# A hybrid decoder layer: part of the 128x128 transposes turned in 32x32 blocks by VectorE and moved by SBUF transfers

## The chip, the cores and the metric

The kernel runs on one core of a Trainium2 chip. Times are device microseconds (us) of one execution. Engines: PE is TensorE, PEld its weight loads, DVE is VectorE, ACT is ScalarE, POOL is GpSimd, SP is SyncE, whose queue issues nearly all transfers of this kernel. L12 is line 12 of the profiled kernel.

## The reference

One layer over 2048 positions of width 1024. Two head groups run side by side on the same projections: four HGRN2 heads (a gated linear recurrence in chunks) and eight attention heads in a sliding window of 128 with a sink logit. Their outputs are concatenated and projected, and a gated MLP with a causal convolution and a last RMSNorm follow. What the change touches:

```python
f = lb + (1.0 - lb) * sigmoid(hf);  log_f = log(f);  k_hg = 1.0 - f
o_hg = hgrn2_chunkwise(q_hg, k_hg, v_hg, log_f)        # per head, 128 keys, 128 values
o_hg = rmsnorm(o_hg, hg_norm_w) * silu(hg)
# attention: block n of 128 queries reads key blocks n-1 and n
dist = qi + ATT_BLOCK - kj;  band = (dist >= 0) & (dist < WINDOW)
p = exp(scores - m);  denom = sum(p) + exp(sink - m)
out = einsum('bnhgqk,bnkhd->bnqhgd', p / denom, vb)
mix = concatenate([o_hg, o_att]);  h = h + mix @ w_out
```

Since the window equals the block, a query sees of its own block the keys up to its own position, and of the previous block exactly the keys after that position: the two masks are complements.

## The kernel before

The 2048 positions go in two halves of 1024. In each, a mix stage (heads, attention) is followed by the output projection, gate and up, and down. Activations lie with features on the 128 partitions and time along the row. Every large product is made of three TensorE matmuls, from a rounded high part and a low part of both factors; a unit of 48 matmuls of 512 columns (8 slices of the width x 3 x two blocks of 512) makes one 128-wide projection for the half. Weights come through three `raw` buffers; ScalarE rounds them to `whi`, VectorE makes the rest `wlo`, two buffers each.

**Attention.** Heads go in four pairs j (one of each key head kv), each pair in two groups g of 512 queries. Stage `qa` projects the queries; `sc` makes the scores `psc`, puts both key blocks into one tile `sc` of 128 keys per query (previous block copied by ScalarE, L405 and L407, own block laid over it by VectorE under the mask `own`, L408), takes the maximum (L411), Exp with sums (L421) and scales (L426). Stages `pv` and `pw` are the value products of group 0 and 1: eight TensorE transposes `ppt` (L435, four for each kv) bring keys onto the partitions, VectorE writes them twice, under the masks `ownT` and `prevT` (L438), and `poT` (L446) sums V of the own block times the one and V of the previous block times the other.

**Heads.** For head h, stage `f` projects and takes Tanh, `q` projects the queries and makes f (VectorE, L472), `l` makes K = 1 - f (VectorE, L475) and works through seven levels of blocks of 1, 2, .. 64 positions (`pdiag`, `plev`), `s` makes the states, `p` the output `po`: ScalarE squares it out of PSUM (L604), VectorE scales it (L612), TensorE transposes it (`pot`, L617, eight for each head), and stage `g` multiplies the gate. Stages `m` split the finished rows into the operands of the output projection.

**Order.** The string `ORDER` gives the sequence in which the stages are traced. A scheduler then places every instruction on its engine by its own estimates and sets the semaphores; each engine, and SyncE's queue, runs its list in order. Tiles of one tag share a number of buffers, and an instruction waits until its buffer is free. A transfer also waits for the eighth transfer before it, whose semaphore it takes.

Of the kernel before, what the change touches and what calls it, by code (L numbers as in the profile page):

```python
# [39 lines left out]
ORDER = ("f0 q0 l0 qa0 v0 s0 p0 sc0 f1 q1 l1 pv0 pw0 qa1 s1 p1 sc1 f2 q2 l2 pv1 pw1 qa2 v1 s2 p2 sc2 f3 q3 l3 "  # L40
         "pv2 pw2 qa3 sc3 s3 p3 g0 pv3 pw3 g1 m4 m5 m6 g2 m0 m1 g3 m7 m2 m3").split()
# [4 lines left out]
VB = 2  # L46


@with_exitstack
def hymba_layer(ctx: ExitStack, tc: tile.TileContext, a: dict, out: bass.AP, rows_out: bass.AP):  # L50
# [29 lines left out]
    ones = cp.tile([P, P], F32, name="ones")  # L80
    nc.vector.memset(ones, 1.0)
# [3 lines left out]
    nc.scalar.activation(warm, ones[:, 0:1], AF.Tanh)  # L85
# [5 lines left out]
    kc = cp.tile([P, 2, P], F32R, name="kcarry")  # L91
    vc = cp.tile([P, P], F32, name="vcarry")
# [6 lines left out]
    def constants():  # L99
# [3 lines left out]
        C.prevT = cp.tile([P, P], F32, name="prevT")  # L103
        for t, op, sgn in ((C.own, ALU.is_ge, 1), (C.ownT, ALU.is_ge, -1), (C.prevT, ALU.is_gt, 1)):
# [229 lines left out]

    def rows(kv):
        return slice(kv * HD, (kv + 1) * HD)

    def att_keys(hf, kv, invb, p):

        KS = p.tile([P, 2, P + HALF], F32R, name="KS")
        V = p.tile([P, 1 + TT, P], F32, name="V")
        if hf:
            nc.vector.tensor_copy(KS[:, :, 0:P], kc)
            nc.vector.tensor_copy(V[:, 0], vc)
        kT, vT = [p.tile([P, HALF], F32, tag="f", name=n, bufs=2) for n in ("kT", "vT")]
        for jj, dst in ((ATT_J, kT), (ATT_J + 1, vT)):
            o = kv[jj - ATT_J]  # L350
            for b, bs in halves():
                nc.vector.tensor_tensor(blocks(dst[:, bs], b), blocks(o[b]), blocks(invb[:, bs]), op=ALU.mult)
                nc.scalar.activation(dst[:, bs], dst[:, bs], AF.Identity, bias=C.battn[:, jj:jj + 1])
        for kv in range(2):
            r, other = rows(kv), rows(1 - kv)
            nc.scalar.copy(KS[r, kv, P:], kT[r])
            nc.vector.tensor_tensor(KS[other, kv, P:], kT[r], KS[r, kv, P:].bitcast(F32), op=ALU.subtract)
        for b in range(NB):
            pv = ps("at", "pv")
            for i in range(4):  # L360
                t0 = (b * 4 + i) * P
                nc.tensor.transpose(pv[:, i * P:(i + 1) * P], vT[:, t0:t0 + P], ident)
            nc.scalar.copy(V[:, 1 + 4 * b:5 + 4 * b].rearrange("p a b -> p (a b)"), pv)
        if hf + 1 < NH:
            nc.vector.tensor_copy(kc, KS[:, :, HALF:HALF + P])
            nc.vector.tensor_copy(vc, V[:, TT])
        return KS, V

    def attend(hf, j, X, invb, KS, V, mix, p):
# [9 lines left out]
        for g in range(NB):  # L379
            sc = p.tile([P, 2, 4, P], F32, tag="sc", name="sc", bufs=2)  # L380
            gs = slice(g * 512, (g + 1) * 512)
            for kv in range(2):
                r, other = rows(kv), rows(1 - kv)

                qh, ql = [p.tile([P, 512], F32R, tag="pp", name=n, bufs=4) for n in ("qh", "ql")]
# [40 lines left out]
            nc.vector.tensor_tensor(sc, sc, den.unsqueeze(3).to_broadcast([P, 2, 4, P]), op=ALU.mult)  # L426
            scs.append(sc)
        yield
        for g, sc in enumerate(scs):
            pm = []  # L430
            for kv in range(2):
                pm.append([p.tile([P, 4, P], F32, tag="pp", name=n, bufs=4) for n in ("po", "pp")])
                pt = ps("at", "ppt")
                for i in range(4):
                    nc.tensor.transpose(pt[:, i * P:(i + 1) * P], sc[:, kv, i], ident)  # L435
                ptv = pt.rearrange("p (i q) -> p i q", i=4)
                for dst, mk in zip(pm[kv], (C.ownT, C.prevT)):
                    nc.vector.tensor_tensor(dst, ptv, mk.unsqueeze(1).to_broadcast([P, 4, P]), op=ALU.mult)  # L438
            oT = ps("at", "poT")
            for i in range(4):  # L440
                n = g * 4 + i
                noprev = hf == 0 and n == 0
                for prev in (0,) if noprev else (1, 0):
                    for kv in (1, 0):
                        r = rows(kv)
                        nc.tensor.matmul(oT[r, i * P:(i + 1) * P], V[:, n + 1 - prev, r], pm[kv][prev][:, i],  # L446
                                         start=noprev or prev == 1, stop=prev == 0)
            gs = slice(g * 512, (g + 1) * 512)
            if j < ATT_J - 1 or "m7" in ORDER:
                nc.scalar.copy(qT[:, gs], oT)  # L450
                mix[4 + j] = qT
            else:
                if g == 0:
                    mix[4 + j] = new_x()
                h, l = mix[4 + j]
                nc.scalar.copy(h[:, gs], oT)
                nc.vector.tensor_tensor(l[:, gs], oT, h[:, gs].bitcast(F32), op=ALU.subtract)
            yield

    def hgrn(hf, h, X, invb, vs, WG, gates, mix, p, fu=None):  # L460
# [11 lines left out]
        nc.vector.tensor_scalar(f, f, C.omlb[:, h:h + 1], C.lb[:, h:h + 1], op0=ALU.mult, op1=ALU.add)  # L472
        yield
        K = p.tile([P, HALF], F32, tag="K", name="K", bufs=2)
        nc.vector.tensor_scalar(K, f, -1.0, 1.0, op0=ALU.mult, op1=ALU.add)  # L475
# [4 lines left out]
        ST = p.tile([P, 2, TT, 64], F32, tag="t4", name="ST", bufs=2)  # L480
# [14 lines left out]
        def gate():  # L495
# [12 lines left out]
        for m in LEVELS:  # L508
# [606 lines left out]
    for hf in range(NH):  # L1115
        X, kv, invb, rs, f0 = nxt
        with ExitStack() as st:
            p = pool(f"mix{hf}", stack=st, reuse_waits="tile")
            KS, V = att_keys(hf, kv, invb, p)
# [4 lines left out]
            pairs = [attend(hf, h, X, invb, KS, V, mix, p) for h in range(HG)]  # L1124
            for name in ORDER:
# [11 lines left out]
                else:  # L1137
                    M[n] = split(mix[n])
# [76 lines left out]
```

## Time and profile before

| | |
|---|---|
| median of 3 runs | 2142.11 us (2142.07 to 2144.53) |
| profiled execution, its own time | 2143.33 us |
| its span, first to last instruction | 2141.6 us |
| mean TensorE clock | 0.999 |
| TensorE busy | 2127.1 us (99%) |
| VectorE busy | 1637.7 us (76%) |
| ScalarE busy | 1025.3 us (48%) |
| transposes `ppt` / `pot` | 128 / 64 |

The two mix stages lie at about 30 to 345 us and 1100 to 1405 us of the span. Busy time counts every record from start to end; TensorE's matmuls overlap one another, so a record is longer than its share of the span. The chain of waits follows the end of the program back to its start, and its pieces do not overlap. A row of waits reads: who waited, for whom, us in total, how often, the longest.

### The profile page before, as it was taken

To read this page: it belongs to the slowest core of one execution; us is meant where nothing else is said; L and a number is where in the kernel's file an instruction comes from. 1 tells how busy PE (TensorE), PEld (TensorE's weight loads), DVE (VectorE), ACT (ScalarE), POOL (GpSimd) and SP (SyncE) were. 2 spreads that over 40 slices of the span, in tenths; PEclk is the share of its full clock that TensorE was granted. 3 is DMA by queue.
4 is the path that set the end of the run, shared out by engine and by line. 5 is a ranking of instruction groups with operands and counts; after the bars stand their busy time and mean duration, and the time that the engine had idled before them with its cause. 6 is when DMAs were issued, how large, how long until landed. Compare 5 with 4: busy or idle time off the path is not lost.

```text
span 2141.6 us, 30162 instructions
## 1 busy us (share of the span) xinstructions
PE 2127.1 (99%) x11719; PEld 1776.1 (83%) x11719; DVE 1637.7 (76%) x2479; ACT 1025.3 (48%) x1826; POOL 18.9 (1%) x45
## 2 busy tenths in 40 slices
PE   8999999999999999999999999999999999999998
PEld 6988888888888888888889898888788888888887
DVE  6677786688887888785875876866888888787765
ACT  5445544464444445345635454544544354444453
POOL 2000000000000000000000000000000000000000
PEclk9999999999999999999999999999999999999999
DMA  4100013313232234964640101042222323259744
GB/s 159 40 31 31 33 38 101 120 65 128 84 128 90 97 118 156 376 244 152 212 138 31 40 21 41 31 146 100 77 99 100 118 84 125 97 179 399 242 148 133
DMA packets 91152, 254.49 MB, mean 119 GB/s; under 512 B 11136, under 2 KB 13952, under 8 KB 91008
## 3 DMA queue, kind: packets, MB, share of 16 engines
q1 hardware_dynamic: 90576, 252.29, 34.3%
q8 instruction: 92, 1.51, 0.3%
q14 instruction: 52, 0.43, 0.1%
q10 hardware_dynamic: 432, 0.27, 0.0%
HBM read 195.37 MB, written 57.15 MB: 118 GB/s over the span
## 4 chain that ended last, share of the span: by engine, by line
PE 97%; DVE 2%; DMA 1%; ACT 0%; issue 0%; SPq 0%; ACTq 0%; DVEq 0%
PE X L779 7%; PE X L778 7%; PE X L777 7%; PE pop L218 7%; PE f L218 4%; PE g L218 4%; PE q L218 4%; PE hq L218 4%; PE Y L779 4%; PE Y L778 4%; PE Y L777 4%; PE pdx L965 3%; PE pdx L966 3%; PE pdx L964 3%; PE pdy L965 3%; PE pdy L966 3%
## 5 line engine op out<-in xcount | busy, mean ns | idle before, releaser
L650 ACT CAST whi<-raw 128x1024 fp32r<-128x1024 f32 x88 | 92.8, 1054 | 114.2 <-PE X L778 73.0
L777 PE MATMUL X<-T,whi 128*128 128x512 f32 x352 | 137.0, 389 | 0.0
L779 PE MATMUL X<-T,wlo 128*128 128x512 f32 x352 | 136.9, 389 | 0.0
L778 PE MATMUL X<-T,whi 128*128 128x512 f32 x352 | 136.9, 389 | 0.0
L848 DVE SCALAR_TENSOR_TENSOR y<-ga,cw,y 128x1024 f32<-128x1024 f32 x88 | 112.6, 1280 | 25.9 <-ACT y L846 25.9
L783 ACT COPY u<-X 128x512 f32<-128x512 f32 x88 | 51.6, 586 | 123.4 <-PE X L779 123.2
L651 DVE TENSOR_TENSOR wlo<-raw,whi 128x1024 fp32r<-128x1024 f32 x88 | 107.3, 1219 | 4.4 <-ACT whi L650 4.4
L199 ACT CAST whi<-raw 128x1024 fp32r<-128x1024 f32 x58 | 60.6, 1050 | 74.4 <-PE pop L218 37.9
L651 DVE TENSOR_TENSOR xld<-raw,xhd 128x1024 fp32r<-128x1024 f32 x72 | 81.1, 1132 | 19.0 <-ACT xhd L650 18.9
L650 ACT CAST xhd<-raw 128x1024 fp32r<-128x1024 f32 x72 | 69.8, 979 | 38.0 <-DMA raw<-act0T 12.7
L218 PE MATMUL pop<-XH,wlo 128*128 128x512 f32 x256 | 81.8, 390 | 0.0
L218 PE MATMUL pop<-XL,whi 128*128 128x512 f32 x256 | 81.5, 390 | 0.0
L218 PE MATMUL pop<-XH,whi 128*128 128x512 f32 x256 | 80.9, 390 | 0.0
L200 DVE TENSOR_TENSOR wlo<-raw,whi 128x1024 fp32r<-128x1024 f32 x58 | 70.5, 1217 | 11.0 <-ACT whi L199 10.9
L777 PEld LDWEIGHTS X<-T,whi 128*128 128x128 f32 x352 | 66.2, 188 | 13.8
L778 PEld LDWEIGHTS X<-T,whi 128*128 128x128 f32 x352 | 66.1, 188 | 13.8
L779 PEld LDWEIGHTS X<-T,wlo 128*128 128x128 f32 x352 | 66.1, 188 | 13.7
L642 PE MATMUL pvv<-whi,XH 128*128 128x256 f32 x256 | 73.2, 287 | 0.0
L643 PE MATMUL pvv<-whi,XL 128*128 128x256 f32 x256 | 72.6, 285 | 0.0
L644 PE MATMUL pvv<-wlo,XH 128*128 128x256 f32 x256 | 72.3, 286 | 0.0
L779 PE MATMUL X<-B,wlo 128*128 128x512 f32 x176 | 69.4, 394 | 0.8 <-DVE wlo L651 0.8
L778 PE MATMUL X<-T,Sh 128*128 128x512 f32 x176 | 68.7, 390 | 1.2 <-DVE T L651 1.2
(383 smaller groups left out, 6350.8 us busy)
## 6 DMA issues: line engine op xcount, KB each, us to landing
wr<-in_w_down SPq DMA_DIRECT2D x90, 512.0 KB, 5.7
raw<-in_w_gate SPq DMA_DIRECT2D x44, 512.0 KB, 3.6
raw<-in_w_up SPq DMA_DIRECT2D x44, 512.0 KB, 3.5
raw<-act0T SPq DMA_DIRECT2D x20, 512.0 KB, 5.8
raw<-act1T SPq DMA_DIRECT2D x20, 512.0 KB, 5.2
act0B<-y SPq DMA_DIRECT2D x33, 256.0 KB, 2.4
act1B<-y SPq DMA_DIRECT2D x33, 256.0 KB, 2.3
raw<-in_w_out SPq DMA_DIRECT2D x16, 512.0 KB, 3.8
```

The costliest lines, as they stand in the source:

```text
L218: nc.tensor.matmul(o[b], w, x[:, bs], start=f, stop=l)
L642: nc.tensor.matmul(o[:, 0:256], xh[:, t], hi[:, c], start=kt == 0, stop=False)
L643: nc.tensor.matmul(o[:, 0:256], xl[:, t], hi[:, c], start=False, stop=False)
L644: nc.tensor.matmul(o[:, 0:256], xh[:, t], lo[:, c], start=False, stop=kt == KT - 1)
L650: nc.scalar.copy(h, src)
L651: return (eng or nc.vector).tensor_tensor(l, src, h.bitcast(F32), op=ALU.subtract)
L777: nc.tensor.matmul(o, wh[:, ws], xh, start=i == 0 and not more, stop=False, skip_group_check=more)
L778: nc.tensor.matmul(o, wh[:, ws], xl, start=False, stop=False, skip_group_check=more)
L779: nc.tensor.matmul(o, wl[:, ws], xh, start=False, stop=i == 3, skip_group_check=more)
L848: nc.vector.scalar_tensor_tensor(y, g[:, w:w + HALF], C.cw[:, ft, w:w + 1], y, op0=ALU.mult, op1=ALU.add)
L965: nc.tensor.matmul(o, wh[:, i, c], al[:, i, cols], start=False, stop=False, skip_group_check=more)
L966: nc.tensor.matmul(o, wl[:, i, c], ah[:, i, cols], start=False, stop=l, skip_group_check=more)
```

## The change

- **Pairs 0 to 2.** The scaled probabilities are turned by VectorE in blocks of 32x32 (STREAM_TRANSPOSE into `turn`, one instruction of 128x1024 per group), and 16 transfers of 32 rows of 1 KB each, on SyncE's queue, put the blocks in their places in `pt`. The 16 `ppt` of a pair and half are gone. Pair 3 keeps them; ScalarE copies them out of PSUM to `pw`.
- **Value product.** With `VD` = V of the own block minus V of the previous block, made once for each half, `poT` sums V of the previous block times the whole, unmasked tile and `VD` times the tile under `ownT`. Only one masked tile is written; `prevT` is gone.
- **Heads 0 to 2.** The scaled output `on` is turned in the same way into the head's row tile; the gate stage reads it there, and the norm weight moves into the split (`m0` to `m2`). Head 3 keeps its `pot`.
- **All heads.** f and K are made by ScalarE. `po` is copied out of PSUM by ScalarE, squared from SBUF, and scaled by one VectorE instruction of 128x1024 in place of two.
- **Buffers.** K has one in place of two; tag `pp` three of 128x1024 in place of four of 128x512; `ST` of heads 0 to 2 lies in the ring of eight row tiles. The keys and values that half 1 needs of half 0 go through DRAM, by four transfers, in place of four copies. The tile `ones` is gone.
- **Order.** `sc` stands ahead of `s` and `p`, and `pv` and `pw` of a pair ahead of the next head's `l`.

```diff
-ORDER = ("f0 q0 l0 qa0 v0 s0 p0 sc0 f1 q1 l1 pv0 pw0 qa1 s1 p1 sc1 f2 q2 l2 pv1 pw1 qa2 v1 s2 p2 sc2 f3 q3 l3 "
...
+ORDER = ("f0 q0 l0 qa0 v0 sc0 s0 p0 f1 q1 pv0 pw0 l1 qa1 sc1 f2 s1 p1 q2 pv1 pw1 l2 qa2 v1 sc2 f3 s2 p2 q3 pv2 "
...
+TURNED_PAIRS = 3
+TURNED_HEADS = 3
...
+    def turned(p, tag, bufs, src, dst):
+
+        t = p.tile([P, 4, 8, 32], F32, tag=tag, name="turn", bufs=bufs)
+        nc.vector.transpose(t, src.rearrange("p n (c j) -> p c n j", j=32))
+        for a in range(4):
+            for c in range(4):
+                nc.sync.dma_start(dst[32 * c:32 * c + 32, a], t[32 * a:32 * a + 32, c])
...
-            nc.vector.tensor_copy(KS[:, :, 0:P], kc)
-            nc.vector.tensor_copy(V[:, 0], vc)
+            nc.sync.dma_start(KS.bitcast(F32)[:, :, 0:P], kc)
+            nc.sync.dma_start(V[:, 0], vc)
...
+        VD = p.tile([P, TT, P], F32, name="VD")
+        if hf:
+            nc.vector.tensor_tensor(VD, V[:, 1:], V[:, 0:TT], op=ALU.subtract)
...
-                qh, ql = [p.tile([P, 512], F32R, tag="pp", name=n, bufs=4) for n in ("qh", "ql")]
+                qx = p.tile([P, 2, 512], F32R, tag="pp", name="qx", bufs=3)
+                qh, ql = qx[:, 0], qx[:, 1]
...
             nc.vector.tensor_tensor(sc, sc, den.unsqueeze(3).to_broadcast([P, 2, 4, P]), op=ALU.mult)
+            if j < TURNED_PAIRS:
+                pt = p.tile([P, 4, 8, 32], F32, tag="sc", name="pt", bufs=2)
+                turned(p, "pp", 3, sc.rearrange("p a b c -> p (a b) c"), pt)
+                sc = pt
...
-                for i in range(4):
-                    nc.tensor.transpose(pt[:, i * P:(i + 1) * P], sc[:, kv, i], ident)
-                ptv = pt.rearrange("p (i q) -> p i q", i=4)
-                for dst, mk in zip(pm[kv], (C.ownT, C.prevT)):
-                    nc.vector.tensor_tensor(dst, ptv, mk.unsqueeze(1).to_broadcast([P, 4, P]), op=ALU.mult)
+            own = p.tile([P, 8, 4, 32], F32, tag="pp", name="po", bufs=3)
+            mk = C.ownT.rearrange("p (a q) -> p a q", a=4).unsqueeze(1)
+            if j < TURNED_PAIRS:
+                whole = sc.rearrange("p a n q -> p n a q")
+                nc.vector.tensor_tensor(own, whole, mk.to_broadcast([P, 8, 4, 32]), op=ALU.mult)
...
-                        nc.tensor.matmul(oT[r, i * P:(i + 1) * P], V[:, n + 1 - prev, r], pm[kv][prev][:, i],
-                                         start=noprev or prev == 1, stop=prev == 0)
+                        nc.tensor.matmul(oT[r, i * P:(i + 1) * P], vv[:, n, r], pr[:, 4 * kv + i],
+                                         start=noprev or w == 0, stop=w == 1)
...
-        nc.vector.tensor_scalar(f, f, C.omlb[:, h:h + 1], C.lb[:, h:h + 1], op0=ALU.mult, op1=ALU.add)
+        nc.scalar.activation(f, f, AF.Identity, scale=C.omlb[:, h:h + 1], bias=C.lb[:, h:h + 1])
...
-        nc.vector.tensor_scalar(K, f, -1.0, 1.0, op0=ALU.mult, op1=ALU.add)
+        nc.scalar.activation(K, f, AF.Identity, scale=-1.0, bias=1.0)
...
-            for i in range(4):
-                c = 4 * b + i
-                nc.scalar.activation(on[:, c], at[i], AF.Square, accum_out=ss[:, c:c + 1])
+            nc.scalar.copy(on[:, 4 * b:4 * b + 4].rearrange("p a b -> p (a b)"), po[b])
+        for c in range(TT):
+            nc.scalar.activation(used[:, c], on[:, c], AF.Square, accum_out=ss[:, c:c + 1])
...
+        nc.vector.tensor_tensor(on, on, rs.unsqueeze(2).to_broadcast([P, TT, P]), op=ALU.mult)
+        if h < TURNED_HEADS:
+            turned(p, "t4", 2, on, q.rearrange("p (a c q) -> p a c q", a=4, c=TT))
+        for b, bs in halves() if h >= TURNED_HEADS else ():
```

How the lists move is shown at three places. First TensorE, half 1, around the output `po` of head 2. Before, between the unit `hq` of head 3 and the unit `q` of pair 3, the eight `ppt` of pair 2's first group stand about it:

```order
L218 MATMUL hq_11764<-XH,wlo 128x512
L435 MATMUL ppt<-ident,sc 128x128
L595 MATMUL po<-v,ST 64x128 x8
L600 MATMUL po<-state,Q 128x128
L600 MATMUL po<-SS,Q 128x128 x3
L595 MATMUL po<-v,ST 64x128 x8
L600 MATMUL po<-SS,Q 128x128 x4
L435 MATMUL ppt<-ident,sc 128x128 x7
L218 MATMUL q_12043<-XH,whi 128x512
```

In the change, within the unit `q` of pair 3 (the scores `psc` are those of pair 2's second group):

```order
L218 MATMUL q_12092<-XH,wlo 128x512
L634 MATMUL po<-v,ST 64x128 x3
L414 MATMUL psc<-KS,qx 128x256 x8
L634 MATMUL po<-v,ST 64x128 x5
L639 MATMUL po<-SS,Q 128x128 x4
L512 MATMUL pdiag<-hg_11893,K 64x64 x7
L471 MATMUL poT<-pt,V 64x128 x2
L512 MATMUL pdiag<-hg_11893,K 64x64 x9
L218 MATMUL q_12091<-XH,whi 128x512
```

No transpose stands there; the first group's value product begins right behind the second group's scores, from `pt`, with a first `poT` of its own in the midst of `pdiag`, and the rest follows later. The second place is SyncE's queue in half 0, around the loads of the second `w_v`. Before:

```order
L198 DMA raw<-in_w_q 128x1024
L198 DMA raw<-in_w_att 128x1024
L198 DMA raw<-in_w_v 128x1024 x2
L198 DMA raw<-in_w_f 128x1024
L198 DMA raw<-in_w_q 128x1024
L198 DMA raw<-in_w_att 128x1024
L198 DMA raw<-in_w_g 128x1024 x4
```

Now:

```order
L198 DMA raw<-in_w_q 128x1024
L198 DMA raw<-in_w_att 128x1024
L341 DMA pt<-turn 32x256 x16
L341 DMA hg_537<-turn 32x256 x16
L198 DMA raw<-in_w_v 128x1024 x2
L341 DMA pt<-turn 32x256 x16
L198 DMA raw<-in_w_f 128x1024
L198 DMA raw<-in_w_q 128x1024
L341 DMA pt<-turn 32x256 x16
L198 DMA raw<-in_w_att 128x1024
L341 DMA pt<-turn 32x256 x16
L341 DMA hg_1358<-turn 32x256 x16
```

Between the weight loads stand groups of 16 transfers, six to `pt` and three to the heads' row tiles (`hg`) in each half. The third place is VectorE, half 0, at the value product of pair 0, second group. Before, each masked copy follows its `ppt`:

```order
L546 COPY_PREDICATED ST<-lmask_289,plev 64x2x128 x2
L526 TENSOR_TENSOR K<-K,F_1360 128x2x128x2
L438 TENSOR_TENSOR po<-ppt,ownT 128x512
L438 TENSOR_TENSOR pp<-ppt,prevT 128x512
L526 TENSOR_TENSOR K<-K,F_1377 128x2x64x4
L527 TENSOR_TENSOR Q<-Q,F_1360 128x2x128x2
L546 COPY_PREDICATED ST<-lmask_295,plev 64x2x64x2 x2
L438 TENSOR_TENSOR po<-ppt,ownT 128x512
L438 TENSOR_TENSOR pp<-ppt,prevT 128x512
```

Now, from the block transpose of that group (`turn`) on:

```order
L338 STREAM_TRANSPOSE turn<-sc 128x1024
L453 TENSOR_TENSOR po<-pt,ownT 128x1024
L565 TENSOR_TENSOR Q<-Q,F_1455 128x2x64x4
L584 COPY_PREDICATED ST<-lmask_297,plev 64x2x32x4 x2
L564 TENSOR_TENSOR K<-K,F_1489 128x2x16x16
L490 TENSOR_TENSOR f<-f_1771,invb 128x512
L490 TENSOR_TENSOR f<-f_1772,invb 128x512
L200 TENSOR_TENSOR wlo<-raw,whi 128x1024
L419 MEMSET sc 128x128 x2
L565 TENSOR_TENSOR Q<-Q,F_1472 128x2x32x8
L584 COPY_PREDICATED ST<-lmask_303,plev 64x2x16x8 x2
L579 TENSOR_TENSOR F_2067<-f 128x512
```

The four masked copies of a group have become one `po<-pt` of 128x1024. The one in the second row is the first group's; the second group's comes after two more rows of `F`, so that thirteen rows stand between its `turn` and it.

More of the change, by code (lines that the diff above doesn't have):

```diff
@@ L84, in hymba_layer @@
     warm = cp.tile([P, 32], F32, name="warm")[:, 0:1]
-    nc.scalar.activation(warm, ones[:, 0:1], AF.Tanh)
+    nc.vector.memset(warm, 1.0)
+    nc.scalar.activation(warm, warm, AF.Tanh)
     nc.gpsimd.memset(ident, 1.0)
@@ L102, in constants @@
         C.ownT = cp.tile([P, P], F32, name="ownT")
-        C.prevT = cp.tile([P, P], F32, name="prevT")
-        for t, op, sgn in ((C.own, ALU.is_ge, 1), (C.ownT, ALU.is_ge, -1), (C.prevT, ALU.is_gt, 1)):
+        for t, op, sgn in ((C.own, ALU.is_ge, 1), (C.ownT, ALU.is_ge, -1)):
             nc.gpsimd.memset(t, 1.0)
@@ L364, in att_keys, with attend @@
         if hf + 1 < NH:
[L365 to L369, printed above, removed]
+            nc.sync.dma_start(kc, KS.bitcast(F32)[:, :, HALF:HALF + P])
+            nc.sync.dma_start(vc, V[:, TT])
+        VD = p.tile([P, TT, P], F32, name="VD")
+        if hf:
+            nc.vector.tensor_tensor(VD, V[:, 1:], V[:, 0:TT], op=ALU.subtract)
+        else:
+            nc.scalar.copy(VD[:, 0], V[:, 1])
+            nc.vector.tensor_tensor(VD[:, 1:], V[:, 2:], V[:, 1:TT], op=ALU.subtract)
+        return KS, V, VD
+    def attend(hf, j, X, invb, KS, V, VD, mix, p):
         o = unit(a["w_att"][j], X, "q")
@@ L429, in attend @@
         for g, sc in enumerate(scs):
[L430 to L433, printed above, removed]
-                for i in range(4):
-                    nc.tensor.transpose(pt[:, i * P:(i + 1) * P], sc[:, kv, i], ident)
-                ptv = pt.rearrange("p (i q) -> p i q", i=4)
-                for dst, mk in zip(pm[kv], (C.ownT, C.prevT)):
-                    nc.vector.tensor_tensor(dst, ptv, mk.unsqueeze(1).to_broadcast([P, 4, P]), op=ALU.mult)
+            own = p.tile([P, 8, 4, 32], F32, tag="pp", name="po", bufs=3)
[3 more added lines that the diff above has]
+                nc.vector.tensor_tensor(own, whole, mk.to_broadcast([P, 8, 4, 32]), op=ALU.mult)
+            else:
+                whole = p.tile([P, 8, 4, 32], F32, tag="pp", name="pw", bufs=3)
+                for kv in range(2):
+                    pt = ps("at", "ppt")
+                    for i in range(4):
+                        nc.tensor.transpose(pt[:, i * P:(i + 1) * P], sc[:, kv, i], ident)
+                    ptv = pt.rearrange("p (n a q) -> p n a q", n=4, a=4)
+                    bs = slice(4 * kv, 4 * kv + 4)
+                    nc.scalar.copy(whole[:, bs].rearrange("p n a q -> p (n a q)"), pt)
+                    nc.vector.tensor_tensor(own[:, bs], ptv, mk.to_broadcast([P, 4, 4, 32]), op=ALU.mult)
             oT = ps("at", "poT")
@@ L1123, in hymba_layer @@
             heads = [hgrn(hf, h, X, invb, vs, WG, gates, mix, p, None if h else f0) for h in range(HG)]
-            pairs = [attend(hf, h, X, invb, KS, V, mix, p) for h in range(HG)]
+            pairs = [attend(hf, h, X, invb, KS, V, VD, mix, p) for h in range(HG)]
             for name in ORDER:
@@ L1137, in hymba_layer @@
                 else:
-                    M[n] = split(mix[n])
+                    M[n] = split(mix[n], C.hgw if n < TURNED_HEADS else None)
             for n in (7, 3):
```

38 lines of the change are left out of this document (23 added, 15 removed).

## The prediction

> **What bounds the kernel now.** I read the page first: its busy shares, then the chain that ended last.
>
> ```profile
> PE 2127.1 (99%) x11719; PEld 1776.1 (83%) x11719; DVE 1637.7 (76%) x2479; ACT 1025.3 (48%) x1826; POOL 18.9 (1%) x45
> PE 97%; DVE 2%; DMA 1%; ACT 0%; issue 0%; SPq 0%; ACTq 0%; DVEq 0%
> ```
>
> TensorE (PE) is busy 99% of the span and carries 97% of the chain. A busy matmul record may still hide a wait, so I read next who TensorE waited for. The view of the waits, for TensorE alone, has four rows in all:
>
> ```profile
> PE kv L218 <- ACT XH L232: 5.5, 1, 5.5
> PE X L778 <- DVE T L651: 1.2, 1, 1.2
> PE X L779 <- DVE wlo L651: 0.8, 2, 0.4
> PE kv L218 <- DVE XL L233: 0.3, 1, 0.3
> ```
>
> None lies in the two mix stages (about 30 to 345 us, and 1100 to 1405 us), where everything changed by the diff stands. Busy time by stretch says the same, and how much room the others have (columns: length, then PE, PEld, DVE, ACT, POOL, clock, DMA share, GB/s):
>
> ```profile
> 80.00:130.00 50.00, 50.00 (x393) 44.80 (x392) 27.19 (x69) 25.98 (x89) 0.52 (x1) 1.00 0.10 33
> 280.00:345.00 65.00, 65.00 (x519) 53.38 (x518) 59.46 (x100) 38.31 (x86) 0.00 (x0) 1.00 0.18 56
> 1220.00:1270.00 50.00, 50.00 (x423) 43.78 (x425) 35.87 (x80) 26.95 (x85) 0.52 (x1) 1.00 0.10 33
> ```
>
> TensorE is full in each; VectorE (DVE) takes 54 to 91% and ScalarE (ACT) 52 to 59%; the clock is 1.00. So an instruction taken from TensorE shortens the span by its own time, as long as nothing that TensorE waits for becomes late. This is a sum over TensorE, and then a check of covers.
>
> **What TensorE loses.** Pairs 0 to 2 lose 16 transposes `ppt` each and half, 96 together; heads 0 to 2 lose 8 `pot` each and half, 48 together: 144 of 128x128. The matmuls of `poT` keep count and shape (two operands for each block and kv, as before). A transpose's share of the chain:
>
> ```profile
> 50.79 0.44 PE pv L362 x4
> 322.59 1.02 PE ppt L435 x8
> 1333.76 1.02 PE pot L617 x8
> L435 PE MATMUL ppt<-ident,sc 128*128 128x128 f32 x128 | 19.4, 277 | 0.0
> ```
>
> The chain's rows follow one another without overlap, so they carry the price: 1.02/8 = 0.1275 us in the groups that go, 0.44/4 = 0.110 us for the same transpose between large matmuls. The record's own 277 ns overlaps its neighbours and is no price. Ends: 144 x 0.110 = 15.8 us and 144 x 0.1275 = 18.4 us. I take 0.12, nearer to the groups that go: **17.3 us**. The Trainium skill, "VectorE: DVE Perf Modes", section on the three transpose paths, gives 390 ns for a 128x128 bf16 transpose on TensorE; by it the sum would be 56 us. That is a rival's figure here, since the chain's row says 127.5.
>
> What TensorE gains: V times `pt` reads `pt` in runs of 32 at a stride. No row shows that; nearest are two kinds of small matmul, one read in order, one in short runs:
>
> ```profile
> 61.01 1.08 PE pdiag L486 x32
> 69.14 0.62 PE plev L520 x16
> ```
>
> 34 against 39 ns: at most 5 ns for each of 180 records, 0.9 us; at least 0. I take 0.5.
>
> **What VectorE and ScalarE get.** Durations by form:
>
> ```profile
> L438 DVE TENSOR_TENSOR po<-ppt,ownT 128x512 f32<-128x512 f32 x32 | 22.0, 687 | 16.2 <-PE ppt L435 16.0
> L438 DVE TENSOR_TENSOR pp<-ppt,prevT 128x512 f32<-128x512 f32 x32 | 21.8, 681 | 0.0
> L472 DVE TENSOR_SCALAR f<-f,omlb,lb 128x1024 f32<-128x1024 f32 x8 | 6.5, 809 | 1.2 <-ACT f L466 1.2
> L475 DVE TENSOR_SCALAR K<-f 128x1024 f32<-128x1024 f32 x8 | 5.5, 690 | 0.1
> L426 DVE TENSOR_TENSOR sc<-sc,den 128x1024 f32<-128x1024 f32 x16 | 19.5, 1220 | 0.2
> L411 DVE TENSOR_REDUCE m<-sc 128x8 f32<-128x1024 f32 x16 | 19.4, 1215 | 0.2
> L408 DVE COPY_PREDICATED sc<-own,psc 128x256 f32<-128x256 uint32 x64 | 27.8, 442 | 7.0 <-ACT sc L405 3.8 <-ACT sc L407 2.7
> L546 DVE COPY_PREDICATED ST<-lmask,plev 64x256 f32<-64x256 uint32 x80 | 44.5, 556 | 2.1
> L232 ACT ACTIVATE XH<-x,nmw 128x1024 fp32r<-128x1024 f32 x15 | 16.7, 1145 | 8.6 <-DMA x<-in_xP 8.5
> L421 ACT ACTIVATE sc<-sc,m 128x128 f32<-128x128 f32 x128 | 49.7, 391 | 0.6 <-DVE m L417 0.5
> L421 ACT ACTIVATION_READ_ACCUMULATOR sc<-sc,m 128x1 f32 x128 | 24.2, 189 | 0.0
> L466 ACT ACTIVATE f<-f 128x512 f32<-128x512 f32 x16 | 9.5, 631 | 0.7 <-DVE f L465 0.6
> ```
>
> VectorE loses 43.8 us of masked copies, 6.5 of `f`, 5.5 of `K`. It gets 12 x 1.22 + 8 x 0.687 = 20.1 for `own`, two `VD` of 1.2, and 18 block transposes. No row shows one: at least 1.22 each (one input, one output of 128x1024, as `sc<-sc,den`), at most twice that; I take 1.22, 22.0 us. Net -11 us, at worst +11, in some 640 us of mix with a third free: it stays off the path. ScalarE gets 16 x 1.145 = 18.3 for `f` and `K`, 24 copies of 128x512 out of PSUM near 0.63 (15) and dearer squares, some 30 us in a half-empty engine. I cost both at nothing; cover and price of failure come next.
>
> **The wait that is added.** In order, a group of one pair now goes: last score copy, maximum, Exp, scaling, block transpose, 16 transfers of 32 KB, then V times `pt` on TensorE and the `own` mask on VectorE. Up to the end of the block transpose: 0.44 + 1.22 + three small ones of 0.17 + 8 x (0.391 + 0.189) + 0.36 + 1.22 + 1.22 = 9.6 us. The transfers' prices are in the rows of SyncE's queue (start, length, what) and in those of waits and landings:
>
> ```profile
> 4.22 5.84 SPq L312 DMA_DIRECT2D x<-in_xP  x6
> 2128.82 3.65 SPq L1098 DMA_DIRECT2D out<-h  x8
> out<-h SPq DMA_DIRECT2D x12, 64.0 KB, 1.7
> SPq L198 <- DVE wlo L200: 465.4, 40, 31.2
> ```
>
> No transfer from SBUF to SBUF is in the trace. Nearest is `out<-h`, 64 KB: eight issued in 3.65 us, 0.456 apart, each landed 1.7 after its issue, so several are in flight. A group: 16 x 0.456 + 1.7 = **9.0 us**. The other end is the six loads of 512 KB at 5.84/6 = 0.97 apart: 16 x 0.97 + 1.7 = 17.2 us. I take 9.0, as the sizes are near. So 18.6 us from the last score to `pt`.
>
> The cover is TensorE's work between a group's last score matmul and its first use of `pt` in the new order. The shortest is half 1, pair 2, first group: 68 matmuls of 512 columns, 16 `psc`, 7 each of `pkn` and `pu`, 24 of `po` and 7 `pdiag`, priced by
>
> ```profile
> 360.89 65.32 PE pop L218 x288
> 1376.41 1.14 PE psc L399 x8
> 1401.81 1.02 PE po L595 x16
> 1402.84 1.09 PE po L600 x8
> 1386.98 1.56 PE pu L576 x14
> ```
>
> 68 x 0.227 = 15.4, and 7.5 for the rest (an order's row of half height is two records): **22.9 us**. The twelve groups, counted alike: 47.9, 29.5, 34.4, 23.8, 38.6, 25.5 in half 0 and 28.9, 29.4, 24.8, 29.0, 22.9, 25.8 in half 1. All exceed 18.6, the tightest by 4.3 us. On VectorE, between a second group's block transpose and its `own`, stand `own` of the first group and some twelve others (half 0, pair 0: 2 of 1.22, 4 of 0.556, 6 of 0.69 and small ones, 9.8 us), so VectorE reaches `own` about when the transfers land. Behind a late `own` stand the next pair's `qx` and a weight split `wlo`; for the split, TensorE still has the other of its two buffers, 48 matmuls. Heads' 16 transfers are needed only by the gate, at the end.
>
> Behind the groups in SyncE's queue stand weight loads. One group holds it 7.3 us; the queue waited 465 us for free weight buffers, so loads run ahead by more. 288 transfers x 0.456 = 131 us of a queue idle most of the mix.
>
> `f` and `K` on ScalarE must be ready when `pdiag` starts, 48 matmuls (10.9 us) after `f`'s unit: two Tanh of 0.63, two of 1.145 and one batch of Exp (4.64) make 8.2 us. Covered. Head 3 keeps its `pot`, behind a longer chain: two copies (1.3), eight squares from SBUF (4.6, priced as Exp), some fourteen small operations (2.4) and one scaling (1.2), 9.5 us; in the new order 47 `pop` matmuls (10.7 us) stand between `po` and `pot`. A miss would cost its own length twice, 1 or 2 us. The carry of K and V through DRAM is four transfers; the first score of half 1 comes 144 matmuls of 512 columns (33 us) after the half's first `f`: hidden.
>
> **The sum.** The profiled execution took 2143.33 us, its span 2141.6. 2143.33 - 17.3 + 0.5 = 2126.5. It lay 1.2 above the median of 2142.11, so **2125.3 us**; own range 2123 to 2128.
>
> **Rivals.**
> - *The transfers are spaced as the large loads are, 0.97 us.* Then `pt` comes 26.8 us after the last score, and five covers fall short: 3.9, 3.0, 2.0, 1.3 and 1.0, 11.2 us given back: 2136.5. For it: the queue has been that slow. Against: `out<-h`, the nearer size. Chance 0.10.
> - *Slower: the sixteen go one after another.* Place: TensorE at the first V times `pt`. 16 x 1.7 = 27.2, with 9.6 36.8 us; ten of the twelve covers fall short, by 2.4 to 13.9, 94 us in all: 2219. It decides from 28 us after the last score, a spacing of 1.04 us, where five shortfalls (5.1, 4.2, 3.2, 2.5, 2.2) eat the 17.3. Against: eight issues in 3.65 us, each of 1.7. For: no transfer of this direction is in the trace. Chance 0.07. The Trainium skill, "DMA: Bandwidth & Descriptors", rules for kernel authors, speaks for it: coalesce small transfers, under 64 KB one pays mostly overhead; with the 2 us of fixed cost of its section on the anatomy of one DMA, paid in a row, a group would take 33 us. The row of overlapping issues speaks against that reading.
> - *ScalarE becomes late.* Two batches of Exp ahead of `f` and `K`: 12.8 us against 10.9, 1.9 us x 8 heads = 15 us: 2140.5, no change. For: both kinds of work now share one in-order engine. Against: half of ScalarE is idle. Chance 0.06.
> - *A transpose's whole record counts*, 277 ns: 144 x 0.277 = 40 us, 2102.7. Against: the chain's rows. Chance 0.02.
>
> **How the numbers follow.** The forecast keeps 0.75. No change means within 0.2%, 4.3 us, about what a measurement of this kernel can tell. Faster: 0.75 + 0.10 + 0.02 = 0.87; same 0.06; slower 0.07. The range of 8 in 10 takes the forecast and most of the first rival, and the upper end of the price: 2121 to 2137.
>
> **What would show it.** Right: `ppt` x32 and `pot` x16 left, TensorE's busy time down by some 17 us and still no row of waits in the mix; 16 transfers of a group issued within 8 us. Wrong: rows of TensorE at `poT` waiting for a transfer or for `own`, or `pdiag` waiting for ScalarE's `K`, a few us each; or `STREAM_TRANSPOSE` above 2.5 us.

## The result and the profile after

The change takes **2129.3 us** (median; 2129.05 to 2129.72), the kernel before 2142.4 beside it: a ratio of 0.9937, 95% interval 0.9920 to 0.9954. It is faster by 13.1 us, where 17 were forecast; 2129.3 lies inside the range of 2121 to 2137 and above the likeliest case's own 2123 to 2128. The profiled execution took 2129.44 us, span 2127.7, clock 0.999.

The page of the change, busy shares and chain; TensorE lost 13.4 us of busy time (2127.1 before), and 144 instructions; VectorE lost 5.3 and ScalarE got 24.7:

```profile
PE 2113.7 (99%) x11575; PEld 1763.0 (83%) x11575; DVE 1632.4 (77%) x2427; ACT 1050.0 (49%) x1855; POOL 16.9 (1%) x43
PE 97%; DVE 2%; DMA 1%; ACT 0%; issue 0%; SPq 0%; ACTq 0%; DVEq 0%
```

All rows of the waits of TensorE:

```profile
PE kv L218 <- ACT XH L232: 5.5, 1, 5.5
PE X L818 <- DVE wlo L690: 0.8, 2, 0.4
PE X L817 <- DVE T L690: 0.5, 1, 0.5
PE kv L218 <- DVE XL L233: 0.3, 1, 0.3
PE poT L471 <- DVE po L463: 0.2, 1, 0.2
```

The only new row is the last, 0.2 us at pair 3. TensorE waits nowhere for a transfer or for ScalarE's `K`. VectorE does wait for transfers, 5.1 us in three places ahead of its mask `po<-pt`, without making TensorE late. So the missing 4 us are not a stall that a row names.

The views of the tiles `turn`, `pt`, `ppt` and `pot` (count, then ns min/median/max, first and last start in us):

```profile
L338 DVE STREAM_TRANSPOSE turn<-sc x12: 1234/1239/1245, 116.1 to 1331.2; 128x1024 f32<-128x1024 f32 x12
L341 SPq DMA_DIRECT2D pt<-turn x192: 507/589/1588, 117.3 to 1341.9; - x192
DMA to landing us min/median/max: 1.8/1.8/3.5
L459 PE MATMUL ppt<-ident,sc x32: 270/272/327, 315.8 to 1408.2; 128*128 128x128 f32 x32
L656 PE MATMUL pot<-ident,on x16: 272/272/273, 357.3 to 1409.1; 128*128 128x128 f32 x16
```

SyncE's queue in the timeline (start, length of the sixteen), two of the groups:

```profile
117.34 10.08 SPq L341 DMA_DIRECT2D pt<-turn  x16
246.31 11.01 SPq L341 DMA_DIRECT2D pt<-turn  x16
```

The block transpose took 1.24 us (1.22 assumed). A transfer from SBUF to SBUF occupies the queue 0.589 us and follows the one before after 10.08/16 = 0.63 to 11.01/16 = 0.69 us, not after 0.456. It lands after 1.8 us (1.7 assumed), so several are in flight, but a group takes some 12.4 us, not 9.0.

The cover that the prediction called tightest (half 1, pair 2, first group) in the timeline: its last scores on TensorE, its transfers, its first use:

```profile
1295.75 0.64 PE L414 MATMUL psc<-KS,qx 128*128 128x256 f32 x4
...
1307.31 10.65 SPq L341 DMA_DIRECT2D pt<-turn  x16
...
1321.85 0.28 PE L471 MATMUL poT<-pt,V 128*64 128x128 f32 x1
```

The scores end at 1296.4, the last transfer lands at 1307.31 + 10.65 + 1.8 = 1319.8, the use comes at 1321.85. So the chain took 23.4 us (18.6 forecast), the cover was 25.5 (22.9 forecast): 2.1 us were left of the forecast's 4.3.

**Where the time is counted from here on.** The gain is best seen between the first matmul of head 0's `f` and the first of the gate and up products (`X`), that is in mix and output projection of a half. In the timeline of the change:

```profile
32.59 0.71 PE L218 MATMUL f<-XH,whi 128*128 128x512 f32 x2
430.08 0.39 PE L816 MATMUL X<-B,whi 128*128 128x512 f32 x1
...
1085.08 0.61 PE L218 MATMUL f<-XH,whi 128*128 128x512 f32 x2
1485.10 0.39 PE L816 MATMUL X<-B,whi 128*128 128x512 f32 x1
```

397.5 us in half 0 and 400.0 in half 1; before, the same two starts are 404.9 and 404.5 us apart. So the mixes gave 7.4 + 4.5 = **11.9 us**. The other 2.0 of the 13.9 between the two spans lie in stretches that the change leaves alone, nearly all behind the second mix (644.7 us before, 642.6 after, 641.8 to 643.4 in the runs below): the profiled execution of before was long there, as its 2143.33 against a median near 2142.4 says too.

### The profile page after: what moved, and what is told of

Read it like the earlier page. It is cut to its first block, busy times and chain, and to the rows that moved or that the text cites. A ratio compares the mean times of both kernels' runs of the same rounds, so it can differ in the third digit from the quotient of the medians.

```text
span 2127.7 us, 30275 instructions
## 1 busy us (share of the span) xinstructions
PE 2113.7 (99%) x11575; PEld 1763.0 (83%) x11575; DVE 1632.4 (77%) x2427; ACT 1050.0 (49%) x1855; POOL 16.9 (1%) x43
## 4 chain that ended last, share of the span: by engine, by line
PE 97%; DVE 2%; DMA 1%; ACT 0%; issue 0%; SPq 0%; ACTq 0%; DVEq 0%
PE X L818 7%; PE X L816 7%; PE X L817 7%; PE pop L218 7%; PE hq L218 4%; PE q L218 4%; PE g L218 4%; PE f L218 4%; PE Y L817 4%; PE Y L818 4%; PE Y L816 4%; PE pdx L1004 3%; PE pdx L1003 3%; PE pdx L1005 3%; PE pdy L1004 3%; PE pdy L1003 3%
```

## The experiments

Each is an edit of the change. "Half-height" is a matmul whose product fills 64 (or 32) of the 128 PSUM partitions: `poT`, `plev`, `pdiag` and the `po<-v` part. A "visit" is one entry of TensorE's list from full height into a run of them; the mix of before has 44 + 41, that of the change 44 + 46 (there `poT` stands in 15 visits in half 1, 10 before). Theory S says that a visit costs time which no wait row shows.

**1. No turning, heads alone, pairs alone.**

```diff
-TURNED_PAIRS = 3
-TURNED_HEADS = 3
+TURNED_PAIRS = 0   # no turning: both 0; heads alone: this one
+TURNED_HEADS = 0   # pairs alone: this one
```

> The change with nothing turned: all 192 transposes stay on TensorE, and every other part of the change is in (V difference, f and K on ScalarE, copies of po, buffers, carry, order). Theory S (what was given back lies in more entries into and out of half-size matmuls, about 0.25 us for a visit, and each transpose removed is worth 0.12): the new order has 89 such visits against 85 before, so some 1 us above before, 2143.4; the turning alone is then worth 14 us. Rival W (the rest costs nothing, and turning gives back 4 us in short waits for pt and own that the trace hides): as before, 2142.4.

> The change with no pair turned, three heads turned: 144 transposes stay. S: 48 x 0.12 = 5.8 us below the run with nothing turned, 2137.6, with 89 visits in both. W: hidden waits belong to the pairs alone, so the heads' whole 5.8 us come off 2142.4: 2136.6.

> The change with three pairs turned, no head: 96 transposes stay, 88 visits. S: 96 x 0.12 = 11.5 us below the run with nothing turned, 2131.9. W: 11.5 less some 4 given back, 2135.

| kernel | us | ratio to before, interval | mix, half 0 / half 1 | visits |
|---|---|---|---|---|
| before | 2142.4 | | 404.9 / 404.5 | 44 + 41 |
| the change | 2129.3 | 0.9937, 0.9920 to 0.9954 | 397.5 / 400.0 | 44 + 46 |
| no turning | 2144.68 | 1.0009, 0.9999 to 1.0018 | 405.7 / 406.9 | 44 + 45 |
| heads alone | 2137.64 | 0.9976, 0.9965 to 0.9986 | 403.7 / 403.0 | 46 + 43 |
| pairs alone | 2139.91 | 0.9986, 0.9976 to 0.9995 | 404.5 / 402.7 | 45 + 43 |

Medians of different sets of runs compare to some 0.4 us: before took 2142.4 to 2142.9 us in the four sets of this document. Without turning, with all the rest of the change in it, the kernel is not faster than before: the gain appears only when the transposes go. Against this kernel the change saves 15.4 us for 144 transposes, 0.107 each (in the mixes 8.2 + 6.8 = 15.0, 0.104). The rest of the change, costed at +0.5, costs 0.8 + 2.4 = 3.1 us in the mixes.

Heads alone gave 7.0 us for 48, more than the 5.8 of the forecast's price. Pairs alone gave 4.8 for 96, where that price makes 11.5, and its rows of waits say where most of it went:

```profile
PE pkn L607 <- DVE K L576: 2.8, 1, 2.8
PE poT L471 <- DVE po L463: 1.0, 1, 1.0
PE pop L218 <- ACT XH L229: 0.8, 1, 0.8
```

4.6 us, for VectorE's `K` and mask above all. With the heads turned too these rows are gone, so the two parts do not add: pairs on top of heads are worth 8.3 us, heads on top of pairs 10.6.

**2. Fewer visits at `poT`: the own block's product first.** `poT<-po,VD` is traced ahead of `poT<-pt,V`; in the trace `poT` then stands in 8 + 8 visits for 11 + 15 (the expectation counted 27).

```diff
-for w, (vv, pr) in enumerate(((V, whole), (VD, own))):
+for w, (vv, pr) in enumerate(((VD, own), (V, whole))):
```

> The change with the two halves of the value product in the other order: VD times the masked tile first, V of the previous block times pt second, so that TensorE's first poT of a group waits for the mask too and a group stands in one piece. The order then has 81 visits to half-size matmuls against 90 in the change (16 runs of poT against 27). S: 9 x 0.25 = 2.3 us faster than the change, 2127.0. W (short waits for late pt and own): the first poT is needed later than pt by a mask of 1.2 us, nothing is gained or up to 1.2 us a group lost: 2129.3 to 2135.

2128.16 us (2128.12 to 2128.63), ratio 0.9932 (0.9917 to 0.9946): 1.1 below the change; the intervals of the two ratios overlap. The mixes: 398.3 and 398.6. Half 1, with 5 visits fewer, gained 1.4; half 0, with 4 fewer, lost 0.8, and has new rows of waits, since the masked tile is now needed first:

```profile
PE poT L471 <- DVE po L453: 0.7, 1, 0.7
PE pot L656 <- DVE on L650: 0.6, 1, 0.6
PE poT L471 <- DVE po L463: 0.5, 1, 0.5
```

**3. The price of a visit, by itself.** 128 float32 products that nothing reads, in four units of the output projection of each half: half-height in pairs ahead of each slice (64 places), half-height in blocks of 16 behind the unit (8 places), and full height in pairs (64 places). The cut below is shortened:

```diff
 for kt in order:                     # a slice
+    for c in range(2):               # block: 16 of them behind the unit instead
+        nc.tensor.matmul(junk[rows(c), 0:P], hi[:, kt * P:kt * P + 64].bitcast(F32), X[kt][0][:, 0:P].bitcast(F32), ...)
+        # full height: junk[:, c * P:(c + 1) * P], hi[:, kt * P:(kt + 1) * P]
     ...                              # its 6 matmuls of 512 columns
```

> The change, with 128 more matmuls of half height (64 of 128 output rows, 128 columns) into a PSUM tile that nothing reads: two behind each of the 8 slices of four units of the output projection in each half, so that they stand between matmuls of 512 columns of full height, at 64 places. The result is the layer's. Their own price by the rows of po<-v (64x128, 0.055 to 0.064 us each): 7 to 8 us. Theory S (each step from full height to half height and back costs TensorE some 0.2 us each way that no wait row shows): 64 places x 0.25 to 0.4 = 16 to 26 us on top, 2129.3 + 7 + 16 to 26 = 2152 to 2162. Rival N (only the instructions count, wherever they stand): 2136 to 2138.

> The same 128 half-height matmuls, but as one run of 16 behind each of the same eight units, so at 8 places in place of 64. S: 2129.3 + 7 + 8 x 0.25 to 0.4 = 2138 to 2140, some 14 to 22 us below the scattered one. N: 2136 to 2138, the same as the scattered one.

> 128 matmuls of full height (128 output rows, 128 columns) in the same 64 places, two by two. Price by the chain's rows of ppt (0.110 to 0.1275 us each): 14 to 16 us. S: no step in height, so 2143 to 2146, below the scattered half-height kernel although each matmul is as long or longer. N: 2143 to 2146 as well, but then above the scattered half-height kernel. If two matmuls set between large ones cost much more than this whatever their height, it is the interruption and not the height, and S falls.

| extra products | us | above the change | longer mix, half 0 / half 1 |
|---|---|---|---|
| half-height, 64 places | 2169.32 (2169.25 to 2169.61) | 40.0 | 19.44 / 19.43 |
| half-height, 8 places | 2145.63 (2145.32 to 2145.96) | 16.3 | 8.48 / 8.48 |
| full height, 64 places | 2159.60 (2159.00 to 2161.16) | 30.3 | 14.72 / 14.75 |

The order is S's: the same 128 instructions cost 23.7 us more at 64 places than at 8 (0.42 for each of 56 visits, the figure of the later expectations). From the mixes, 32 pairs and 32 visits make 19.44, 32 pairs and 4 visits 8.48: a visit costs 10.96/28 = **0.39 us**, a pair 0.216. Full height shows no such step: 14.73/64 = 0.230 each. My prices for the products were wrong in all three (7 to 8 and 14 to 16 us expected): a full-height product of 128 columns cost 0.230 us, twice a transpose of the same shape, and two half-height ones together about as much as one. The trace shows why: each of these products leaves two records, 256 for 128, where a transpose leaves one.

```profile
L217 PE MATMUL junk<-XH,whi x256: 270/274/275, 375.5 to 1502.0; 128*128 128x128 f32 x128
```

The starts of these records lie 0.109 us apart, as those of `ppt` do in the kernel before. A pair's four make 0.44 of the 0.46 us that it cost, so the interruption of the large matmuls by itself costs next to nothing, and the height is what counts.

The weight loads (PEld) in the timeline show the step; in brackets the idle time ahead. First the scattered half-height pairs (a pair is four loads), then the block of 16:

```profile
375.96 0.20 PEld L217 LDWEIGHTS junk<-XH,whi 128*64 128x64 f32 x4 [0.35 <-ACT h L747]
376.32 0.30 PEld L221 LDWEIGHTS pop<-XH,whi 128*128 128x128 f32 x2 [0.17 <-issue]
376.67 0.42 PEld L221 LDWEIGHTS pop<-XL,whi 128*128 128x128 f32 x2
```

```profile
386.77 1.73 PEld L222 LDWEIGHTS junk<-XH,whi 128*64 128x64 f32 x32 [0.35 <-PE pop L219]
388.67 0.30 PEld L219 LDWEIGHTS pop<-XH,whi 128*128 128x128 f32 x2 [0.17 <-ACT sq L252]
```

The full-height pairs, with no bracket:

```profile
377.09 0.64 PEld L217 LDWEIGHTS junk<-XH,whi 128*128 128x128 f32 x4
377.65 0.30 PEld L221 LDWEIGHTS pop<-XH,whi 128*128 128x128 f32 x2
```

At a change of height the weight loads stand idle for 0.35 to 0.37 us on the way in and 0.17 on the way out, at each of the 64 and of the 8 places, once for each run whatever its length; ahead of a full-height pair it is 0.04 us. The releasers named in the brackets differ from place to place, and the idle time does not follow them. The mixes' own visits show the step too: in the start times, with the mean spacing of each form taken off, the two edges of a visit hold 0.22 us in before, without turning and in the change, and 0.23 for the visits added here; the rest of the 0.39 must lie in the records next to an edge. The Trainium skill, "TensorEngine Tiling (Array Packing)", section Key Properties, says that changing the tiling mode drains TensorE, and gives no time for it; these rows agree, and the price here is 0.39 us for in and out. The prediction did not use it.

**4. Twice the transfers.** Each transfer in two of 16 KB.

```diff
-nc.sync.dma_start(dst[32 * c:32 * c + 32, a], t[32 * a:32 * a + 32, c])
+for s in (slice(0, 4), slice(4, 8)):
+    nc.sync.dma_start(dst[32 * c:32 * c + 32, a, s], t[32 * a:32 * a + 32, c, s])
```

> The change with each of the 16 transfers of a turned tile cut in two, 32 transfers of 16 KB. The change's trace has them 0.63 to 0.69 us apart and landed 1.8 us after issue: 32 x 0.66 + 1.8 = 22.9 us, 32.5 us from the last score to pt. Cover theory C (the prediction's: a group's pt must be there after 22.9 to 47.9 us of TensorE's other work): eight of the twelve covers (22.9, 23.8, 24.8, 25.5, 25.8, 28.9, 29.0, 29.4) and 29.5 fall short, 9.6 + 8.7 + 7.7 + 7.0 + 6.7 + 3.6 + 3.5 + 3.1 + 3.0 = 52.9 us if the order stays: up to 2182, and less where one wait covers the next; rows of TensorE at poT waiting for a DMA. Rival H (the transfers are hidden whatever their number, or a split transfer issues in half the time): 2129 to 2131, no such rows.

2177.15 us (2176.59 to 2179.47): 47.9 above the change, where adding up the covers gave 52.9. A group in SyncE's queue:

```profile
117.29 21.03 SPq L342 DMA_DIRECT2D pt<-turn  x32
```

The first rows of TensorE's waits, and two stretches of the timeline (columns as in the prediction's table of stretches; the third from the right is the granted clock):

```profile
PE poT L472 <- ACT pw L463: 6.1, 2, 5.1
PE kv L218 <- ACT XH L232: 5.8, 2, 5.3
PE poT L472 <- DMA pt<-turn: 5.4, 1, 5.4
PE ppt L460 <- DVE sc L442: 5.3, 1, 5.3
PE poT L472 <- DVE po L464: 5.1, 4, 2.3
```

```profile
360.00:380.00 20.00, 10.44 (x86) 8.58 (x85) 9.53 (x21) 10.68 (x43) 0.00 (x0) 0.74 0.00 1
1400.00:1420.00 20.00, 13.19 (x89) 10.23 (x87) 5.63 (x8) 8.22 (x14) 0.00 (x0) 0.83 0.12 27
```

Half the size does not issue faster: 21.03/32 = 0.66 us. The transfers are hidden only as long as their number fits the cover. One row of TensorE names the transfer itself. The others (`pw`, `sc`, `po`) are read as work that the late groups pushed back: VectorE sat idle ahead of its masks `po<-pt` for 11.8 us until a `pt` and for 9.0 us until a head's transfers had landed. That the total came so near to the sum of the covers is in part luck. The mixes are 22.9 and 25.6 us longer, where the covers of the two halves give 18.7 and 34.2. TensorE's rows of waits in the mixes make 34.2 us of these 48.5; most of the rest is slower work, some 14 us more of busy time for the same matmuls, in stretches behind the waits where the granted clock was 0.74 to 0.91 (1.00 all through the change's mixes).

**5. No transfers, and f and K on VectorE.** First, VectorE's transpose writes straight into `pt`; second, the old two lines.

```diff
-turned(p, "pp", 3, sc..., pt)
+nc.vector.transpose(pt, ...)                      # no transfers

-nc.scalar.activation(f, f, AF.Identity, scale=C.omlb[:, h:h + 1], bias=C.lb[:, h:h + 1])
-nc.scalar.activation(K, f, AF.Identity, scale=-1.0, bias=1.0)
+nc.vector.tensor_scalar(f, f, C.omlb[:, h:h + 1], C.lb[:, h:h + 1], op0=ALU.mult, op1=ALU.add)
+nc.vector.tensor_scalar(K, f, -1.0, 1.0, op0=ALU.mult, op1=ALU.add)   # f and K on VectorE
```

> The change without the 192 transfers of pairs 0 to 2: VectorE's block transpose writes straight into the tile that the value product reads. The blocks are then not moved to their places, so the attention of pairs 0 to 2 is not the reference's; every instruction but the transfers stays. 89 visits for 90. Hidden at nothing, as the prediction costed them: 2128.9 to 2129.3. Rival T (192 transfers take something from TensorE or VectorE that no wait row shows, which is where the missing 4 us went): 2125 to 2126.

2126.73 us (2126.10 to 2127.12), between the two expectations. The mixes: 397.1 and 399.1, 0.4 and 0.9 less; one visit fewer is worth 0.4 of that. So 192 transfers took at most 2.6 us, some 1 us of it in the mixes. The rest lies behind them, where also kernels with the same code differ by 1 to 2 us. Since the scheduler places the list anew when the latency goes, this is a bound and not a price.

> The change with f and K made by VectorE again (16 instructions moved from one engine to the other, TensorE's work the same). The scheduler's list for TensorE then enters half-height matmuls 96 times for 90 (48 and 48 for 44 and 46). S: 6 x 0.42 = 2.5 more, 2131.8, more in half 0 (4 visits, 1.7) than in half 1 (2, 0.8), and no new row of waits of more than 1 us. N, the prediction's step (f and K cost nothing on either engine): 2129.3.

2138.61 us (2136.43 to 2140.34): 9.3 above the change, where S gave 2.5 and the prediction's "nothing" 0. Rows of TensorE's waits:

```profile
PE poT L471 <- DVE po L463: 4.1, 3, 2.4
PE poT L471 <- ACT pw L462: 1.0, 1, 1.0
PE poT L471 <- issue: 0.4, 1, 0.4
```

16 instructions of some 0.75 us, 12 us in all, on an engine that is busy 77% of the span: 5.5 us came back as waits of TensorE at pair 3, whose mask VectorE makes just before. With six visits more (2.3), and 1.3 us at a granted clock of 0.84 and 0.81 between 357 and 367 us, this makes 9.1 of the 10.0 by which the mixes are longer (404.7 and 402.9). Neither theory had it: with the transposes turned, moving `f` and `K` to ScalarE is a part of the gain.

**6. `po` grouped, and everything that takes visits away.** The 16 half-height `po<-v` of a head stand together, the full-height products behind them; the second kernel adds experiment 2 and turns the fourth head.

```diff
 for b in range(NB):
     ...                              # 8 po<-v
+for b in range(NB):
     ...                              # 4 po<-state, po<-SS
```

> The change, with the 16 half-height po<-v of a head's two blocks traced one behind the other and the full-height products of state and SS behind them, in place of 8, 4, 8, 4. No instruction is added, removed or resized. TensorE's list then enters half-height matmuls 83 times in the mix in place of 90 (half 0: 41 for 44, half 1: 42 for 46). S at the 0.42 us of a visit that scattered against block gave (23.7 us over 56 visits): 7 x 0.42 = 2.9 us less, 2126.4, of it 1.3 in half 0 and 1.7 in half 1. N (only the instructions count): 2129.3. If po's copy by ScalarE comes later through the new order and head 3's pot waits for it, 2130 to 2132 with a row of waits at pot.

> The change with po grouped as in the run beside it, the value product's own block first (the run 'own first'), and all four heads turned, so that 16 more pot are gone. TensorE enters half-height matmuls 77 times for 90, and 32 transposes are left. S: 13 x 0.42 = 5.5 less, 16 transposes at 0.104 (the change against itself without turning: 15.4 us over 144, 0.107) to 0.146 (heads alone: 7.0 over 48) = 1.7 to 2.3 less, 2121.5 to 2122.1. N: 2127.0 to 2127.6. Slower than both if the gate of head 3, last in the mix, waits for its 16 transfers: 16 x 0.66 + 1.8 = 12.4 us behind its scaling, twice, up to 2134, with a row of TensorE at pop waiting for a split of head 3.

Grouped: 2129.85 us (2128.86 to 2129.94), no gain. Half 0 went to 396.7, 0.8 less (1.2 by three visits). Half 1 went to 402.3, 2.3 *more*, where four visits fewer should have given 1.6. Its rows name 2.0 us of waits, and right behind them the granted clock is lower:

```profile
PE poT L471 <- ACT pw L462: 1.7, 1, 1.7
PE poT L471 <- DVE po L463: 0.3, 1, 0.3
```

```profile
1409.00:1414.00 5.00, 5.00 (x35) 4.10 (x32) 4.50 (x16) 2.69 (x3) 0.00 (x0) 0.66 0.00 0
```

Five microseconds of full work at 0.66 lose 1.7 us. Without the waits and this loss half 1 would be at 398.6, 1.4 less than the change, so both halves then give back nearly what their visits are priced at (0.8 of 1.2 and 1.4 of 1.6). Why the clock fell here is not shown: the longer wait of pairs alone, 2.8 us, has no such stretch behind it.

Fewest visits: 2127.68 us (2126.86 to 2128.92), ratio 0.9931 (0.9916 to 0.9946), where S gave 2121.5 to 2122.1 and N 2127.0 to 2127.6. It is the lowest of the kernels that compute the layer, yet not to be told from experiment 2. Its waits grew to 4.1 us in the mix:

```profile
PE poT L471 <- DVE po L463: 3.6, 2, 1.9
PE pop L218 <- ACT XH L232: 0.5, 1, 0.5
```

Less these waits, the mixes are 5.5 us shorter than the change's, where 13 visits and 16 transposes at the measured prices make 6.7. So most of what the prices give was there, and waits, for the mask of pair 3 above all, took more than half of it back.

## Why the prediction was right, and 4 us short

The direction, the bound (TensorE, by its own sum) and the covers held. By its steps, in the mixes, where -17.3 + 0.5 = -16.8 us were forecast and -11.9 measured:

- **The price of a transpose was mis-sized.** 0.12 was taken, between 0.110 and 0.1275; taking 144 away from the same kernel gave 0.104 in the mixes (0.107 by the medians, or with the one visit that the change has more taken out). That is 2.3 us of the 4.9. The lower end was near; the upper end, from the groups that go, was not their price. Both of its rows follow half-height matmuls in the chain of before:

```profile
321.98 0.62 PE plev L534 x16
1333.00 0.77 PE poT L446 x13
```

  The starts of `ppt` and of `pot` within a group lie 0.109 us apart there (the median of all groups). Eight make 0.87 us; the other 0.15 us of the row of 1.02 is the step out of half height ahead of them, and the list had no fewer visits when the transposes went.
- **"The matmuls of `poT` keep count and shape", +0.5, was the other miss**: the change without turning costs 3.1 us, not 0.5. Count and shape are indeed the same, and the strided reads of `pt`, for which the 0.5 stood, are not in the 3.1: the kernel without turning reads no `pt`. In the change the starts of `poT` records lie 54.5 ns apart (median) with `pt` as with `pw`, and so they do before, so these reads cost nothing that shows. What changed is the list: four visits more in half 1 without turning, five with it, at 0.39 us each 1.6 to 2.0 us. The price of a visit is shown (experiment 3). That it is what half 1 lost is supported: with five visits fewer (experiment 2) half 1 gave back 1.4 in spite of new waits, and with four fewer (`po` grouped) 1.4 once its waits and the lower clock are taken out. The other 1.5 us, 0.8 in either half, are open.
- **The correction of 1.2 us** for the profiled execution of before was too small: 2.0 us of its length lay in stretches outside the mixes. This made up 0.8 of the 4.9 by luck, which leaves the 4 us (4.1 by these rounded figures).
- **A group of transfers: 9.0 us** was mis-sized. The nearest row, `out<-h`, gave a spacing of 0.456; measured 0.63 to 0.69, a group 12.4. It cost nothing, because the cover was also longer than counted (25.5 against 22.9). By the counted cover the chain of 23.4 us would have been 0.5 too late, so that the step held at its tightest place was luck. The rival "spaced as the large loads are" lay on the other side of the truth: 0.97 was too slow, and no cover fell short.
- **That the cover decides** was right, and experiment 4 shows it from the other side: with 32 transfers 47.9 us were lost, of which TensorE's waits name 34.2. The 52.9 of the same arithmetic was right in size, and near only by the help of the lower clock. The slower rival of serial transfers was priced rightly in kind; its premise was wrong, since each of several transfers in flight landed in 1.8 us. The 33 us for a group, from the fixed cost that the Trainium skill, "DMA: Bandwidth & Descriptors", section on the anatomy of one DMA, gives for a transfer that GpSimd issues (these are SyncE's), stand against 12.4 measured: a cost of that size is there (1.8 us to landing), but it does not add up over the group.
- **VectorE "stays off the path", with up to 11 us more at nothing**, was wrong as a general statement. It got 5.3 us less work, not 11 less, and held; but with 12 us more (experiment 5) TensorE lost 9.3. Idle shares of a whole mix did not show how tight the masks of pair 3 are.
- **ScalarE late** did not come about: no row at `pdiag`. `f` and `K` took 1.24 and 1.06 us (1.145 assumed); ScalarE got 24.7 us, not 30.

```profile
L497 ACT ACTIVATE f<-f,lb,omlb 128x1024 f32<-128x1024 f32 x8 | 9.9, 1242 | 0.2
L500 ACT ACTIVATE K<-f 128x1024 f32<-128x1024 f32 x8 | 8.5, 1063 | 0.1
```

- **A whole record for a transpose** (277 ns) is ruled out by 0.104 to 0.107. So is a sum by the 390 ns that the Trainium skill, "VectorE: DVE Perf Modes", section on the three transpose paths, gives for a bf16 transpose on TensorE.
- Of what would show the steps right: `ppt` x32 and `pot` x16 came, and no wait rows of more than 0.2 us in the mix. TensorE's busy time fell by 13.4, not 17. The 16 transfers took 10 to 11 us to issue, not 8.

Across before, the change and eight edits of it (all but experiments 3 and 4), the two mixes less 0.104 for each transpose left, less the named waits and less the 1.7 and 1.3 us lost at a lower clock in two of them spread over 7.2 us. With 0.39 for each visit, a price that was not fitted to these kernels, they spread over 2.2. Part of that gain comes from one kernel, `f` and `K` on VectorE; without it the spreads are 4.1 and 2.2. So some 2 us of what the scheduler's list does stay unpriced, and a sum over instructions, visits and waits is no better than that here.

## What to carry to other kernels

Where TensorE is full, price an instruction by the spacing of the starts in a run of its kind; a row of the chain can hold a step at its edge as well (0.1275 against 0.109 us here). Then compare the two lists for matmuls that use part of the array's height: each entry into a run of them costs a step that no wait row and no count of instructions shows. When an operation is replaced by transfers, count their issue on the queue, one by one, against the work that stands between: here halving the size did not quicken the issue, and doubling the number cost 48 us. An engine with a quarter of its time free can still be on the path at one place, and putting some work back on it is a quick test. Behind waits, look at the granted clock too: it can take as much as a wait does, and no wait row shows it.

## What the runs showed of the hardware

- A change between full-height and half-height matmuls left the weight loads idle for 0.35 us going in and 0.17 us coming out, 0.39 us net for both; two half-height float32 products of 128 columns took 0.216 us together, one full-height product 0.230. Such a product leaves two records, a transpose one, with starts 0.109 us apart in both.
- A transfer from SBUF to SBUF of 32 rows occupied SyncE's queue about 0.59 us and followed the last after 0.63 to 0.69 us, with 32 KB as with 16 KB, and landed 1.8 us after its issue.
- VectorE turned 128x1024 float32 in blocks of 32x32 in 1.24 us, as long as its multiplication of the same size (1.20 to 1.22).
- Behind waits of TensorE the granted clock fell in some runs: to 0.66 over 5 us behind 2.0 us of waits (`po` grouped), to 0.74 to 0.91 in four stretches of 20 us with 32 transfers. Behind a wait of 2.8 us (pairs alone) it stayed at 1.00.
